# A new order of the attention's matmuls, and a new end of the last layer, in a two-layer decoder trunk

## The chip, the core and the metric

The kernel runs on one core of one Trainium2 chip. TensorE (PE) multiplies, and loads weights beside it (PEld); VectorE (DVE), ScalarE (ACT) and GpSimd (POOL) do the elementwise work; SyncE (SP) issues nearly all transfers. The metric is the device time of one execution in microseconds. A matmul reads its operands from on-chip memory (SBUF) and adds into one of the eight banks of PSUM, 128 partitions of 512 f32 numbers each.

## The reference

All arithmetic is float32, on 1024 tokens of width 1024, in two layers:

```python
def hybrid_layer(x, ...):
    fq, fk, fv, f_logit, rq, rk, rv, rg = split(x @ w_in)
    # 8 forgetting-attention heads of 64: causal softmax, one bias per key and query
    logits = q @ k.T * scale + (c_i[:, None] - c[None, :])
    fox_out = softmax(where(causal, logits, -inf)) @ v
    # 4 retention heads of 128, rotary, chunkwise, group norm, silu gate
    mix = concat([fox_out, ret_out]) @ w_out
    x = layernorm(ALPHA * x + mix, ln1_g, ln1_b)
    ff = square(relu(x @ w_ff1)) @ w_ff2           # 1024 -> 4096 -> 1024
    return layernorm(ALPHA * x + ff, ln2_g, ln2_b)
```

## The kernel before

**Products.** Each f32 operand is split into a high part (`hi`, a cast on ACT) and the rest (`lo`, a subtraction on DVE); a product is three matmuls: lo·hi, hi·lo, hi·hi. The helper `split` (L334 the cast, L335 the subtraction) does it nearly everywhere. Both feed-forward matmuls are done in seven block products (a Winograd form of Strassen's scheme).

**Attention.** For each of 8 heads and 4 query blocks of 256 tokens, three kinds of work stand on PE: F, the scores of one chunk (two matmuls into a `qk` bank, L744; there are two such banks); B, transposes of the probabilities of one pair of key blocks (three or four, L774, into one of two `tr` banks); V, four matmuls of those with the values (L793, into a `pv` bank). Between F and B lie on DVE a fused add and row minimum (`sc,mx<-qk`, L751), on ACT the exponential (L758), on DVE a reciprocal (L760), on POOL the scaling (L761). Between B and V lie the split's cast on ACT and its subtraction on DVE (`pt<-tr` and `pt<-tr,pt`), into three buffers for each part (`PT_BUFS`). X is filler that depends on none of this: three matmuls of the later heads' q and k projection, or of the output projection (L417), or four transposes of retention (L442). PE runs the four kinds in the order that `attention_order()` writes ahead of time, since PE takes its instructions in order and the stage lies in a `manual_schedule` of PE. That function is a small planner with its own clock and its own servers for DVE, ACT and POOL. A piece counts as ready some spare time after its data is expected: `MARGIN` (1.2 us) for B and V, half of it for F. Of the pieces that are ready it takes V, then B, then F, then X; X goes first only while fewer X have been placed than `goal` wants at that count of F (the table `marks`; `FIRST` X ahead of the first F). Both layers use the same order. The order on DVE, ACT and SP is made by the framework's scheduler; there too each engine takes its instructions in order.

**The end.** `feed_forward_out` runs seven products over the same 16 operands each (`PRODUCTS`: 1, 6, 2, 7, 5, 4, 3). `Operands.ahead` loads an operand (two transfers of 256 KB into an `est` buffer; four of these) and splits it into `ehi` and `elo` (rings of six). The last product adds into four banks (`tr`, `tr`, `pv`, `pv`; one for each of the last four token tiles) in groups of `E_GROUP` = 4 operands: four operands for bank 0, the same four for bank 1, and so on. For each of the four token tiles `add` (L1354) then adds the bank to the residual, and `finish` does two `bn_stats` (L1324, one for each half of the row), `bn_aggr` and the norm. `layernorm` (L466): (z − mean)·g on DVE (L469), variance plus epsilon and its power −1/2 on POOL (L471, L473), then times that plus b on DVE (L474). The last token tile has its own `layernorm_halves`, with the row in two halves over ACT, DVE and POOL (L481 to L488). The group order of the last product is not held by `manual_schedule`, so the scheduler may mix groups.

Of the kernel before, what the change touches and what calls it, by code (L numbers as in the profile page):

```python
# [2 lines left out]

# [10 lines left out]
AF = mybir.ActivationFunctionType  # L14
ALU = mybir.AluOpType
# [13 lines left out]
EPS = 1e-5  # L29
# [20 lines left out]
QK_STEPS = 36  # L50
LATE = "WWWWRR" + 6 * "WWR" + 8 * "W"
SLACK = 4
FIRST = 30
LANDING = 9.0
RET_LANDING = 12.0
MARGIN = 1.2


def _consts():
# [31 lines left out]
def attention_order():  # L91
# [35 lines left out]
    rest_from = [never]  # L127

    def goal(f):
        marks = ((0, FIRST), (16, 46), (40, 74), (64, 109), (len(chunks), last_x))  # L130
        for (f0, x0), (f1, x1) in zip(marks, marks[1:]):
            if f <= f1:
                return x0 + (x1 - x0) * (f - f0) / (f1 - f0)
# [7 lines left out]
    while nf < len(chunks) or nb < len(turns) or nv < nb:  # L141
        run(t)
        found = {}
        if nv < nb and nv in pt_ready:
            found["V"] = pt_ready[nv] + MARGIN
            i, jp = turns[nv]
            if jp == 0 and steps[i][1] % 2 == 0:
                found["V"] = max(found["V"], pv_free[(i // 2) % 2])
        if nb < len(turns) and nb - nv < PT_BUFS:
            i, jp = turns[nb]  # L150
            qq = steps[i][1]
            if all((i, rb) in prob for rb in (2 * qq, 2 * qq + 1)):
                found["B"] = MARGIN + max(tr_free[nb % 2], *(prob[(i, rb)] for rb in (2 * qq, 2 * qq + 1)))
        if nf < len(chunks):
            i = chunks[nf][0]
            done = ends[turns[nb][0] - 1] if turns[min(nb, len(turns) - 1)][0] else 0
            if nf - done < DEPTH and (i < 4 or nb >= len(turns) or turns[nb][0] > i - 4) and steps[i][0] in landed:
                found["F"] = MARGIN / 2 + max(qk_free[nf % 2], landed[steps[i][0]])
        if nx < last_x and nx < goal(nf) + SLACK:
            if nx < qk_x:  # L160
                found["X"] = mm_free[(nx // 9) % 2] if nx % 9 == 0 else 0.0
# [91 lines left out]
def hybrid_trunk(ctx: ExitStack, tc, x, w_in, w_out, w_ff1, w_ff2, ln1_g, ln1_b, ln2_g, ln2_b,  # L253
# [222 lines left out]
    def layernorm_halves(z, st, g, b, dst):  # L476
        mv = small([P, 1, 2], "mv")
        V.bn_aggr(mv[:, 0, :], st)
        rs, nb = rstd_of(mv, 1)
        h0, h1 = slice(0, D // 2), slice(D // 2, D)  # L480
        A.activation(z[:, h0], z[:, h0], AF.Identity, bias=nb, scale=rs)  # L481
        V.tensor_scalar(z[:, h1], z[:, h1], rs, nb, op0=ALU.mult, op1=ALU.add)
        V.tensor_tensor(z[:, h1], z[:, h1], g[:, h1], op=ALU.mult)
        G.tensor_tensor(z[:, h0], z[:, h0], g[:, h0], op=ALU.mult)
        V.tensor_tensor(z[:, h1], z[:, h1], b[:, h1], op=ALU.add)
        SP.dma_start(dst[:, h1], z[:, h1])
        V.tensor_tensor(z[:, h0], z[:, h0], b[:, h0], op=ALU.add)
        SP.dma_start(dst[:, h0], z[:, h0])  # L488

    def rows(ap, n):  # L490
        return ap.partition_broadcast(n)
# [719 lines left out]
    class Operands:  # L1211
        def __init__(self, l):
            w2 = w_ff2[l].rearrange("(j m p) (h d) -> j p m h d", m=2, p=P, h=2)
            self.left = {1: 0, 2: 1, 4: 2, 5: 3, 6: 4, 7: 5, 3: 6}
            self.right = {1: lambda j: w2[j][:, 0, 0], 2: lambda j: w2[j][:, 1, 0], 3: lambda j: w2[j][:, 1, 1],
                          4: lambda j: t_d[j][:, 3], 5: lambda j: t_d[j][:, 0], 6: lambda j: t_d[j][:, 1],
                          7: lambda j: t_d[j][:, 2]}
            self.todo = [(p, j) for p in PRODUCTS for j in range(NM // 2)]
            self.ready, self.sent, self.pool = {}, 0, None

        def ahead(self, n):
            while self.sent < min(len(self.todo), n):
                p, j = self.todo[self.sent]
                early = self.sent < 2 * E_EARLY
                if early and self.sent % 4 < 2:
                    st = wp.tile([P, 2, 512], F32, tag="wst", name=nm("est"), bufs=2)
                elif early:
                    if self.sent % 2 == 0:
                        self.two = act.tile([P, 4, 512], F32, tag="act", name=nm("est"))
                    st = self.two[:, 2 * (self.sent % 2) : 2 * (self.sent % 2) + 2, :]  # L1230
                else:
                    st = self.pool.tile([P, 2, 512], F32, tag="est", name=nm("est"), bufs=E_STAGE)
                SP.dma_start(st[:, 0, :], h_d[j][:, self.left[p], :])
                SP.dma_start(st[:, 1, :], self.right[p](j))
                if self.sent < E_EARLY:
                    both = act.tile([P, 4, 512], F32R, tag="act", name=nm("eboth"))
                    hi, lo = both[:, 0:2, :], both[:, 2:4, :]
                elif early:
                    hi = wp.tile([P, 2, 512], F32R, tag="whi", name=nm("ehi"))
                    lo = wp.tile([P, 2, 512], F32R, tag="wlo", name=nm("elo"))  # L1240
                else:
                    hi = self.pool.tile([P, 2, 512], F32R, tag="ehi", name=nm("ehi"), bufs=E_RING)
                    lo = self.pool.tile([P, 2, 512], F32R, tag="elo", name=nm("elo"), bufs=E_RING)
                split(hi, lo, st)
                self.ready[(p, j)] = (hi, lo)
                self.sent += 1
# [5 lines left out]
    def feed_forward_out(l, operands, nxt):  # L1252
# [37 lines left out]
        def triple(ps, i, ops, first, last):  # L1290
            for n, (x_, y) in enumerate(((1, 0), (0, 1), (0, 0))):
                PE.matmul(ps, ops[x_][:, 0, i * P : i * P + P], ops[y][:, 1, :], start=first and n == 0,  # L1292
                          stop=last and n == 2, skip_group_check=True)

        def product(p, ps, first, last, done):
            group = E_GROUP if p == PRODUCTS[-1] else 1
            for j0 in range(0, NJ, group):
                ops = [operands.take(p, j) for j in range(j0, j0 + group)]
                for j in range(j0, j0 + group):
                    if (p, j) in hooks:  # L1300
                        hooks.pop((p, j))(ops[j - j0][0][0:1, :, 0:1].bitcast(F32))
                for i in range(4):
                    for j, o in enumerate(ops):
                        triple(ps[i], i, o, first and j0 + j == 0, last and j0 + j == NJ - 1)
                    if j0 + group == NJ:
                        done(i)
                    if group > 1 or i == 3:
                        tick()
# [11 lines left out]
        def finish(tt):  # L1320
            zt = acc[tt // 2][:, tt % 2, :]
            g, b = last
            for dh in range(2):
                V.bn_stats(stats[:, tt, dh, :], zt[:, 512 * dh : 512 * dh + 512])  # L1324
            if nxt is None and tt == NT - 1:
                layernorm_halves(zt, stats[:, tt], g, b, out[tt * P : tt * P + P, :])
# [77 lines left out]
```

## Time and profile before

| | us |
|---|---|
| median of 3 runs | 2372.41 (2370.77 to 2372.44) |
| profiled execution | 2368.65, of it span 2366.8 |
| PE busy in the span | 2328.8 (98%) |
| DVE, ACT, POOL busy | 1512.2, 1017.7, 396.5 |
| attention, layer 0 and layer 1 | 304.5 to 500 and 1480 to 1676 in the span |
| last product on PE | 2307.1 to 2350.8 |

In the profile PE is all but full, so only stretches in which it has nothing to do can be won, or the tail after its last matmul. A matmul row shows 0.39 us for 512 columns, while the next one starts 0.227 us later (twelve of them take 2.72 us in the chain of waits): the rows overlap by some 0.16 us, and by as much every gap between two rows is too short. "Idle before" is what such a gap is called there.

### The profile page before, as it was taken

What the parts mean: (1) busy time and instruction counts of PE and PEld (TensorE: products, weight loads), DVE (VectorE), ACT (ScalarE), POOL (GpSimd) and SP (SyncE); (2) the same over time, 40 slices, a digit from 0 to 9 for tenths busy, and PEclk for the clock granted to TensorE, in tenths of its full rate; (3) what the DMA queues carried; (4) which work ended last, traced back from release to release, by engine and by line L of the source; (5) the groups of instructions that cost most, each with busy time, mean ns of one, the idle gap of its engine ahead of it and who ended that gap; (6) DMA issues with size and microseconds to landing.
All of it is one profiled execution on the core that took longest, in us unless ns stands there. A gap on an engine that the chain in (4) does not pass through costs nothing.

```text
span 2366.8 us, 32263 instructions
## 1 busy us (share of the span) xinstructions
PE 2328.8 (98%) x11696; PEld 1973.3 (83%) x11696; DVE 1512.2 (64%) x2805; ACT 1017.7 (43%) x1555; POOL 396.5 (17%) x533
## 2 busy tenths in 40 slices
PE   8999999999999999999999999999999999999997
PEld 8888888888888888888898888888888888888885
DVE  4655367756776657655745653777577766676557
ACT  4122256627445444334322222666274454443331
POOL 0232256401000000000202323554000000000003
PEclk9999999999999999999999999999999999999998
DMA  7566776323454458667455667672334544686663
GB/s 251 184 213 210 233 218 200 113 90 126 141 200 175 155 205 297 214 199 236 144 175 196 214 210 243 179 226 87 117 107 162 207 147 147 236 290 219 193 195 142
DMA packets 242159, 443.50 MB, mean 187 GB/s; under 512 B 22080, under 2 KB 126528, under 8 KB 233808
## 3 DMA queue, kind: packets, MB, share of 16 engines
q1 hardware_dynamic: 239696, 433.06, 55.9%
q10 hardware_dynamic: 2304, 8.39, 0.9%
q8 instruction: 92, 1.51, 0.3%
q14 instruction: 67, 0.55, 0.1%
HBM read 302.90 MB, written 138.48 MB: 186 GB/s over the span
## 4 chain that ended last, share of the span: by engine, by line
PE 86%; DVE 4%; DMA 4%; issue 3%; ACT 1%; SPq 1%; POOL 1%; ACTq 0%; DVEq 0%; POOLq 0%
PE mm L417 14%; PE qk L417 10%; PE qk L1082 9%; PE pv L1082 7%; PE tr L1292 7%; PE pv L1292 7%; PE qk L1292 6%; PE mm L1292 6%; PE mm L1082 5%; PE tr L1082 4%; PE pv L793 2%; PE qk L744 2%; PE tr L774 2%; PE tr L417 1%; PE pv L417 1%
## 5 line engine op out<-in xcount | busy, mean ns | idle before, releaser
L335 DVE TENSOR_TENSOR elo<-est,ehi 128x1024 fp32r<-128x1024 f32 x216 | 260.9, 1222 | 180.1 <-ACT ehi L334 179.7
L334 ACT CAST ehi<-est 128x1024 fp32r<-128x1024 f32 x216 | 226.5, 1054 | 342.6 <-PE pv L1292 117.5
L471 POOL TENSOR_SCALAR sd<-mv 128x1 f32<-128x1 f32 x15 | 13.9, 928 | 1202.3 <-DVE mv L468 1202.0
L417 PE MATMUL mm<-whi,act 128*128 128x512 f32 (+1 forms) x656 | 204.0, 373 | 7.6 <-ACT whi L334 5.4
L1082 PE MATMUL qk<-xop,whi 128*128 128x512 f32 x624 | 192.2, 389 | 0.0
L334 ACT CAST whi<-wst 128x512 fp32r<-128x512 f32 (+1 forms) x140 | 115.9, 831 | 158.4 <-DMA wst<-in_w_in_dram 27.4
L417 PE MATMUL qk<-whi,act 128*128 128x512 f32 (+1 forms) x560 | 172.7, 374 | 0.8 <-DVE act L335 0.8
L335 DVE TENSOR_TENSOR wlo<-wst,whi 128x512 fp32r<-128x512 f32 (+1 forms) x140 | 133.3, 954 | 38.4 <-ACT whi L334 37.9
L1082 PE MATMUL pv<-xop,whi 128*128 128x512 f32 x512 | 157.6, 389 | 0.0
L417 PEld LDWEIGHTS mm<-whi,act 128*128 128x128 f32 x656 | 119.8, 190 | 27.4 <-ACT whi L334 5.4
L1082 PEld LDWEIGHTS qk<-xop,whi 128*128 128x128 f32 x624 | 117.1, 188 | 24.2
L1082 PE MATMUL mm<-xop,whi 128*128 128x512 f32 x400 | 123.2, 389 | 0.0
L758 ACT ACTIVATE sc<-sc,mx 128x128 f32<-128x128 f32 (+7 forms) x128 | 99.4, 777 | 53.2 <-DVE mx L751 42.0
L1082 PE MATMUL qk<-xop,wlo 128*128 128x512 f32 x312 | 121.7, 390 | 0.0
L417 PE MATMUL mm<-wlo,act 128*128 128x512 f32 (+1 forms) x328 | 121.3, 370 | 0.0
L335 DVE TENSOR_TENSOR pt<-tr,pt 128x512 fp32r<-128x512 f32 (+1 forms) x160 | 100.7, 632 | 29.0 <-ACT pt L334 27.4
L417 PE MATMUL mm<-act,whi 128*128 128x512 f32 x384 | 119.1, 391 | 0.0
L417 PEld LDWEIGHTS qk<-whi,act 128*128 128x128 f32 x560 | 102.6, 190 | 17.8 <-DVE act L335 1.0
L1082 PEld LDWEIGHTS pv<-xop,whi 128*128 128x128 f32 x512 | 96.1, 188 | 20.0
L761 POOL TENSOR_SCALAR sc<-sc,ri 128x128 f32<-128x128 f32 (+7 forms) x128 | 98.4, 774 | 84.9 <-DVE ri L760 69.7
L334 ACT CAST pt<-tr 128x512 fp32r<-128x512 f32 (+1 forms) x160 | 85.3, 543 | 62.3 <-PE tr L774 61.4
L793 PE MATMUL pv<-pt,vp 128*128 128x256 f32 (+1 forms) x640 | 105.1, 283 | 6.6 <-DVE pt L335 6.6
(286 smaller groups left out, 5929.6 us busy)
## 6 DMA issues: line engine op xcount, KB each, us to landing
est<-h_d SPq DMA_DIRECT2D x224, 256.0 KB, 3.9
wst<-in_w_ff_dram SPq DMA_DIRECT2D x78, 512.0 KB, 4.2
wr<-in_w_ff_dram SPq DMA_DIRECT2D x32, 1024.0 KB, 5.2
t_d<-ts SPq DMA_DIRECT2D x32, 1024.0 KB, 4.3
h_d<-hs SPq DMA_DIRECT2D x32, 1024.0 KB, 5.1
est<-t_d SPq DMA_DIRECT2D x128, 256.0 KB, 3.9
h_d<-rest SPq DMA_DIRECT2D x32, 768.0 KB, 5.5
est<-in_w_ff_dram SPq DMA_DIRECT2D x96, 256.0 KB, 4.9
```

What stands on the lines that cost most here:

```text
L334: A.copy(hi, src)
L335: V.tensor_tensor(lo, src, hi.bitcast(F32), op=ALU.subtract)
L417: PE.matmul(ps, lhs(a, k), rhs(b, k), start=first and i == 0 and j == 0, stop=last and i == n - 1 and j == 2)
L471: G.tensor_scalar(sd, mv[:, :, 1], EPS, 1.0, op0=ALU.add, op1=ALU.mult)
L744: PE.matmul(ps[:, 0:w], qs[:, rb * P : rb * P + P], ks[part][:, c0 : c0 + w], start=part == 0, stop=part == 1)
L758: A.activation(sc[:, 0:ne], sc[:, 0:ne], AF.Exp, bias=mx, scale=-1.0, accum_out=sm)
L761: G.tensor_scalar(sc[:, 0:ne], sc[:, 0:ne], ri, 1.0, op0=ALU.mult, op1=ALU.mult)
L774: PE.transpose(tr[:, 2 * i + rb, :], probs[rb][:, j * P : j * P + P], ident)
L793: PE.matmul(ob[:, c + f * P : c + 256], vp[:, js[i], :], pt[b][:, 2 * i + f : 2 * i + 2, :], start=qq % 2 == 0 and jp == 0 and n == 0 and ...
L1082: PE.matmul(ps, ops[p][a][:, k, :], right[p][b][:, k, :], start=first and k == 0 and n == 0, stop=last and k == 3 and n == 2, skip_group_c ...
L1292: PE.matmul(ps, ops[x_][:, 0, i * P : i * P + P], ops[y][:, 1, :], start=first and n == 0, stop=last and n == 2, skip_group_check=True)
```

## The change

Three things.

1. In the planner each kind has a spare time of its own: F 0.83 us (0.6 before), B 1.54 (1.2), V 2.78 (1.2). `FIRST` is 32 (30), and `goal` wants 57 X by the 16th F (46) and 83 by the 40th (74). The count of matmuls is the same.
2. In the last layer, the last product has groups of 4, 4 and 8 operands in place of four of 4. While the group of eight runs, PE's order is held by `manual_schedule`. The eight operands ahead of the last four are split into one buffer of the pool `act` each (`eboth`) in place of the rings.
3. The norm of the last token tile is written like `layernorm`, with the last step in two halves; ACT's and POOL's share of the row is gone. The `bn_stats` of the first half of tiles 4 to 7 is written further ahead, after product 4.

```diff
-FIRST = 30
+MARK1, MARK2 = 57, 83
+FIRST = 32
-MARGIN = 1.2
+MARGIN_F = 0.83
+MARGIN_B = 1.54
+MARGIN_V = 2.78
...
-        marks = ((0, FIRST), (16, 46), (40, 74), (64, 109), (len(chunks), last_x))
+        marks = ((0, FIRST), (16, MARK1), (40, MARK2), (64, 109), (len(chunks), last_x))
...
-        rs, nb = rstd_of(mv, 1)
-        h0, h1 = slice(0, D // 2), slice(D // 2, D)
-        A.activation(z[:, h0], z[:, h0], AF.Identity, bias=nb, scale=rs)
-        V.tensor_scalar(z[:, h1], z[:, h1], rs, nb, op0=ALU.mult, op1=ALU.add)
-        V.tensor_tensor(z[:, h1], z[:, h1], g[:, h1], op=ALU.mult)
-        G.tensor_tensor(z[:, h0], z[:, h0], g[:, h0], op=ALU.mult)
-        V.tensor_tensor(z[:, h1], z[:, h1], b[:, h1], op=ALU.add)
-        SP.dma_start(dst[:, h1], z[:, h1])
-        V.tensor_tensor(z[:, h0], z[:, h0], b[:, h0], op=ALU.add)
-        SP.dma_start(dst[:, h0], z[:, h0])
+        sd = small([P, 2], "sd")[:, 0:1]
+        G.tensor_scalar(sd, mv[:, :, 1], EPS, 1.0, op0=ALU.add, op1=ALU.mult)
+        rs = small([P, 2], "rs")[:, 0:1]
+        G.tensor_tensor(rs, sd, half[:, 0:1], op=ALU.pow)
+        V.scalar_tensor_tensor(z, z, mv[:, 0, 0:1], g, op0=ALU.subtract, op1=ALU.mult)
+        for h in (slice(D // 2, D), slice(0, D // 2)):
+            V.scalar_tensor_tensor(z[:, h], z[:, h], rs, b[:, h], op0=ALU.mult, op1=ALU.add)
+            SP.dma_start(dst[:, h], z[:, h])
...
-                if self.sent < E_EARLY:
+                if self.sent < E_EARLY or self.closing and 4 < len(self.todo) - self.sent <= E_CLOSE + 4:
                     both = act.tile([P, 4, 512], F32R, tag="act", name=nm("eboth"))
...
-            group = E_GROUP if p == PRODUCTS[-1] else 1
-            for j0 in range(0, NJ, group):
+            sizes = [E_GROUP] * (NJ // E_GROUP) if p == PRODUCTS[-1] else [1] * NJ
+            if nxt is None and p == PRODUCTS[-1]:
+                sizes = [E_GROUP] * ((NJ - E_CLOSE) // E_GROUP) + [E_CLOSE]
...
+                with tc.manual_schedule(engines={mybir.EngineType.PE}) if group == E_CLOSE else nullcontext():
+                    for i in range(4):
+                        for j, o in enumerate(ops):
+                            triple(ps[i], i, o, first and j0 + j == 0, last and j0 + j == NJ - 1)
...
+        if nxt is None:
+            for i in range(4):
+                V.bn_stats(stats[:, i + 4, 0, :], z(1, i, 0)[0])
```

**PE, near the end of layer 0's attention: turn 78 (the 79th of 80 pairs of B and V).** Before, B into `tr_5529` is followed at once by the V ahead of it, by the next B, and by its own V (`pt_5534`, `pt_5535`).

```order
L774 MATMUL tr_5529<-cst,sc_5381 128x128
L774 MATMUL tr_5529<-cst,sc_5411 128x128
L793 MATMUL pv_5486<-pt_5521,vp_4950 128x256
L793 MATMUL pv_5486<-pt_5522,vp_4950 128x256
L793 MATMUL pv_5486<-pt_5521,vp_4950 128x256
L793 MATMUL pv_5486<-pt_5522,vp_4950 128x256
L774 MATMUL tr_5542<-cst,sc_5411 128x128
L774 MATMUL tr_5542<-cst,sc_5381 128x128
L774 MATMUL tr_5542<-cst,sc_5411 128x128
L793 MATMUL pv_5486<-pt_5534,vp_4950 128x256
L793 MATMUL pv_5486<-pt_5535,vp_4950 128x256
```

Now B of the same turn goes into `tr_5525`, and fourteen matmuls of the output projection, the next B and another V stand ahead of its V (`pt_5530`, `pt_5531`).

```order
L776 MATMUL tr_5525<-cst,sc_5407 128x128
L795 MATMUL pv_5494<-pt_5504,vp_4957 128x256
...
L421 MATMUL pv_5597<-wlo_4706,mix_4588 128x512
L421 MATMUL pv_5597<-whi_4705,mix_4588 128x512
L776 MATMUL tr_5538<-cst,sc_5407 128x128
L776 MATMUL tr_5538<-cst,sc_5377 128x128
...
L795 MATMUL pv_5494<-pt_5517,vp_4957 128x256
L795 MATMUL pv_5494<-pt_5518,vp_4957 128x256
...
L795 MATMUL pv_5494<-pt_5530,vp_4957 128x256
L795 MATMUL pv_5494<-pt_5531,vp_4957 128x256
```

What moved: the V of a turn stands further behind its own B. Over the 80 turns of a layer, the pairs with less than 2 us of PE work between the last transpose and the first matmul that reads the `lo` part were 8, and are 1. From a row block's last score to its first transpose, the pairs with under 4.5 us were 2 of 32, and are none. The first eight F had 8 X between them, and have 11; behind the 16th F there were 95 X, and are 85; behind the 64th 33, and are 30.

**PE, the end of the last product.** Before, the last four operands' matmuls are mixed: bank 0 (`tr_20525`) and bank 1 (`tr_20526`) end eighteen and fifteen matmuls before the last; six matmuls of bank 2 and nine of bank 3 (the `pv` banks) stand behind.

```order
L1292 MATMUL tr_20525<-ehi_21369,elo_21370 128x512
L1292 MATMUL tr_20525<-elo_21370,ehi_21369 128x512
L1292 MATMUL tr_20525<-ehi_21369 128x512
L1292 MATMUL tr_20526<-ehi_21369,elo_21370 128x512
L1292 MATMUL tr_20526<-elo_21370,ehi_21369 128x512
L1292 MATMUL tr_20526<-ehi_21369 128x512
L1292 MATMUL pv_20527<-ehi_21362,elo_21363 128x512
```

Now a bank gets all 24 matmuls of the eight operands before the next one starts (`eboth` three matmuls to a row).

```order
L1295 MATMUL tr_20525<-ehi_21365,elo_21366 128x512
L1295 MATMUL tr_20525<-elo_21366,ehi_21365 128x512
L1295 MATMUL tr_20525<-ehi_21365 128x512
L1295 MATMUL tr_20526<-eboth_21261 128x512 x3
L1295 MATMUL tr_20526<-eboth_21267 128x512 x3
L1295 MATMUL tr_20526<-eboth_21273 128x512 x3
L1295 MATMUL tr_20526<-eboth_21279 128x512 x3
L1295 MATMUL tr_20526<-ehi_21344,elo_21345 128x512
```

What moved: bank 0 is complete 72 matmuls before the last, bank 1 48 and bank 2 24.

**DVE, the end of the program.** Before:

```order
L474 SCALAR_TENSOR_TENSOR acc_19401<-acc_19401,rs_21465,lb_20257 128x1024
L1324 BN_STATS stats_19253<-acc_19485 128x6
L469 SCALAR_TENSOR_TENSOR acc_19485<-acc_19485,mv_21484,lg_20256 128x1024
L478 BN_AGGR mv_21508<-stats_19253 128x2
L474 SCALAR_TENSOR_TENSOR acc_19485<-acc_19485,rs_21489,lb_20257 128x1024
L463 SCALAR_TENSOR_TENSOR nb_21514<-mv_21508,rs_21512 128x1
L482 TENSOR_SCALAR acc_19485<-acc_19485,rs_21512,nb_21514 128x512
L483 TENSOR_TENSOR acc_19485<-acc_19485,lg_20256 128x512
L485 TENSOR_TENSOR acc_19485<-acc_19485,lb_20257 128x512
L487 TENSOR_TENSOR acc_19485<-acc_19485,lb_20257 128x512
```

and now:

```order
L478 SCALAR_TENSOR_TENSOR acc_19485<-acc_19485,rs_21472,lb_20257 128x1024
L1363 TENSOR_TENSOR acc_19485<-acc_19485,pv_20528 128x512
L1333 BN_STATS stats_19253<-acc_19485 128x6
L482 BN_AGGR mv_21502<-stats_19253 128x2
L487 SCALAR_TENSOR_TENSOR acc_19485<-acc_19485,mv_21502,lg_20256 128x1024
L489 SCALAR_TENSOR_TENSOR acc_19485<-acc_19485,rs_21506,lb_20257 128x512 x2
```

What moved: the norms of the last four tiles stand one behind the other, each behind its own bank's addition, where those of two tiles at a time were mixed. The `bn_stats` that the source now writes further ahead already stood after product 4 in the scheduler's order, and does not move.

More of the change, by code (lines that the diff above doesn't have):

```diff
@@ L1 @@
-from contextlib import ExitStack
+from contextlib import ExitStack, nullcontext
 from itertools import chain
@@ L38 @@
 E_EARLY = 4
+E_CLOSE = 8
 LEAD = 7
@@ L144, in attention_order @@
         if nv < nb and nv in pt_ready:
-            found["V"] = pt_ready[nv] + MARGIN
+            found["V"] = pt_ready[nv] + MARGIN_V
             i, jp = turns[nv]
@@ L152, in attention_order @@
             if all((i, rb) in prob for rb in (2 * qq, 2 * qq + 1)):
-                found["B"] = MARGIN + max(tr_free[nb % 2], *(prob[(i, rb)] for rb in (2 * qq, 2 * qq + 1)))
+                found["B"] = MARGIN_B + max(tr_free[nb % 2], *(prob[(i, rb)] for rb in (2 * qq, 2 * qq + 1)))
         if nf < len(chunks):
@@ L157, in attention_order @@
             if nf - done < DEPTH and (i < 4 or nb >= len(turns) or turns[nb][0] > i - 4) and steps[i][0] in landed:
-                found["F"] = MARGIN / 2 + max(qk_free[nf % 2], landed[steps[i][0]])
+                found["F"] = MARGIN_F + max(qk_free[nf % 2], landed[steps[i][0]])
         if nx < last_x and nx < goal(nf) + SLACK:
@@ L1219, in __init__ @@
             self.ready, self.sent, self.pool = {}, 0, None
+            self.closing = l == L - 1
         def ahead(self, n):
@@ L1295, in product @@
         def product(p, ps, first, last, done):
-            group = E_GROUP if p == PRODUCTS[-1] else 1
-            for j0 in range(0, NJ, group):
+            sizes = [E_GROUP] * (NJ // E_GROUP) if p == PRODUCTS[-1] else [1] * NJ
+            if nxt is None and p == PRODUCTS[-1]:
+                sizes = [E_GROUP] * ((NJ - E_CLOSE) // E_GROUP) + [E_CLOSE]
+            j0 = -sizes[0]
+            for before, group in zip([sizes[0]] + sizes, sizes):
+                j0 += before
                 ops = [operands.take(p, j) for j in range(j0, j0 + group)]
@@ L1301, in product @@
                         hooks.pop((p, j))(ops[j - j0][0][0:1, :, 0:1].bitcast(F32))
[L1302 to L1308, printed above, removed]
+                with tc.manual_schedule(engines={mybir.EngineType.PE}) if group == E_CLOSE else nullcontext():
+                    for i in range(4):
+                        for j, o in enumerate(ops):
+                            triple(ps[i], i, o, first and j0 + j == 0, last and j0 + j == NJ - 1)
+                        if j0 + group == NJ:
+                            done(i)
+                        if group > 1 or i == 3:
+                            for _ in range(group // E_GROUP or 1):
+                                tick()
         def z(half, i, dh):
@@ L1322, in finish @@
             g, b = last
-            for dh in range(2):
+            for dh in range(0 if nxt is not None or tt < 4 else 1, 2):
                 V.bn_stats(stats[:, tt, dh, :], zt[:, 512 * dh : 512 * dh + 512])
```

## The prediction

> **What bounds the kernel now.** I read the page's busy shares first, then the table by stretches, then who waited for whom on PE in the two attention stretches, and the chain of waits for the end.
>
> ```profile
> span 2366.8 us, 32263 instructions
> PE 2328.8 (98%) x11696; PEld 1973.3 (83%) x11696; DVE 1512.2 (64%) x2805; ACT 1017.7 (43%) x1555; POOL 396.5 (17%) x533
> ```
>
> PE bounds it: 38 us of the span are without a matmul. The stretches that the change touches hold 29 of these (columns: stretch, its length, busy time of PE, PEld, DVE, ACT, POOL, clock, DMA share, GB/s).
>
> ```profile
> 304.50:500.00 195.50, 189.06 (x1176) 167.34 (x1175) 140.00 (x430) 121.56 (x255) 95.83 (x127) 1.00 0.51 148
> 1480.00:1676.00 196.00, 189.43 (x1177) 167.46 (x1176) 140.04 (x430) 122.07 (x255) 94.47 (x127) 1.00 0.50 147
> 2330.00:2367.00 37.00, 20.82 (x92) 16.89 (x90) 20.96 (x27) 3.87 (x4) 8.03 (x9) 0.83 0.26 104
> ```
>
> Attention leaves PE idle for 6.4 us in layer 0 and 6.6 in layer 1. Who ended that idle time (total us, times, longest), layer 0:
>
> ```profile
> PE pv L793 <- DVE pt L335: 3.3, 6, 1.9
> PE tr L774 <- POOL sc L761: 1.4, 2, 1.2
> PE qk L744 <- DVE mx L751: 1.1, 3, 0.6
> PE mm L417 <- DVE act L335: 0.5, 1, 0.5
> ```
>
> Layer 1 gives the same four numbers. So about half is V waiting for its split, then B for POOL's scaling, then F for a score bank. The end is another case. The chain of waits follows PE's last matmuls into DVE and does not come back:
>
> ```profile
> 2339.95 2.72 PE tr L1292 x12
> ...
> 2346.78 1.37 DVE acc L1354 x2
> ```
>
> and PE's last row is
>
> ```profile
> 2350.44 0.39 PE L1292 MATMUL pv<-ehi 128*128 128x512 f32 x1
> ```
>
> PE is through at 2350.83. From there to the end of the span stand 15.97 us in which DVE, POOL and one transfer work off four token tiles.
>
> **The attention order.** It removes no matmul and adds none; it moves V away from its B. What a V needs is seen best near the end of layer 0, where the engines have little else to do:
>
> ```profile
> 493.12 0.60 PE L774 MATMUL tr<-cst,sc 128*128 128x128 f32 x4
> 493.76 0.59 ACT L334 CAST pt<-tr 128x512 fp32r<-128x512 f32 x1 [3.32 <-PE tr L774]
> 494.38 1.25 DVE L335 TENSOR_TENSOR pt<-tr,pt 128x512 fp32r<-128x512 f32 x2 [3.22 <-ACT pt L334]
> 494.40 0.38 PE L793 MATMUL pv<-pt,vp 128*128 128x256 f32 x1
> 495.12 0.74 PE L793 MATMUL pv<-pt,vp 128*128 128x256 f32 x4 [0.34 <-DVE pt L335]
> ```
>
> The last of the four transposes gives way to the next matmul at about 493.5; ACT casts until 494.35, DVE subtracts for 0.65, and the matmul that reads `lo` starts at 495.12: 1.6 us, with empty queues. With a full DVE queue it is more; the longest wait of all is
>
> ```profile
> 365.21 1.22 DVE L335 TENSOR_TENSOR wlo<-wst,whi 128x1024 fp32r<-128x1024 f32 x1
> 366.47 0.69 DVE L807 TENSOR_TENSOR ot<-ot,pv 64x512 f32<-64x512 f32 x1
> 367.19 1.16 DVE L335 TENSOR_TENSOR pt<-tr,pt 128x512 fp32r<-128x512 f32 x2
> 367.94 0.74 PE L793 MATMUL pv<-pt,vp 128*128 128x256 f32 x4 [1.92 <-DVE pt L335]
> ```
>
> where a weight's split and an output's addition stand ahead. Here PE had some 2.8 us of other work and waited about 2 more, so this turn would have needed 4.8. In the compiled order I counted PE's work between B and the `lo` reader, with PE's start-to-start spacing: under 2 us (the 1.6 and a little queue) stood 8 of the 80 V of a layer, now 1; the turn above has 5.4 in place of 2.8. I take seven eighths of the V waits as gone. A wait costs more than its idle time, since the row before it covers 0.16 us of it (0.39 long against 2.72/12 = 0.227): 3.3 + 6 × 0.16 = 4.3 us, so 3.7 won. For B: 1.4 + 2 × 0.16 = 1.7; both pairs under 4.5 us of cover are gone, but POOL's chain is the long one and B now also has more X ahead of it only at the start; I take half, 0.9. For F: 1.1 + 3 × 0.16 = 1.6, and the cover hardly grows; a quarter, 0.4. The wait of X for the retention split (0.5) I leave. That makes 5.0 a layer, **10.0 us** for both. What hides the deferred V is X and F; DVE has 140 of 195.5 us, so it has room. Bounds: nothing won (each wait returns elsewhere), or all of it, 6.3 + 6.5 (layer 1 has 0.2 more in B) + 25 × 0.16 = 16.8 us.
>
> **The end, first part: does PE end at the same time?** It has the same 192 matmuls. Its group of eight starts after 96 of them:
>
> ```profile
> 2307.14 0.39 PE L1292 MATMUL tr<-ehi,elo 128*128 128x512 f32 x1
> ```
>
> 2307.14 + 96 × 0.227 = 2328.9, and then wants a fresh operand every 0.68 us: the eighth by 2333.7. This is the step that can go wrong, since a split takes DVE 1.2 us. In DVE's new order the last split has ten splits, four additions, four `bn_stats`, four `bn_aggr` and five long norm steps from the same addition on that started at 2305.30. That row, and the groups of 2305 to 2347:
>
> ```profile
> 2305.30 0.69 DVE L1354 TENSOR_TENSOR acc<-acc,mm 128x512 f32<-128x512 f32 x1 [1.09 <-PE mm L1292]
> ```
>
> ```profile
> L335 DVE TENSOR_TENSOR elo<-est,ehi 128x1024 fp32r<-128x1024 f32 x12 | 14.4, 1220 | 7.0 <-ACT ehi L334 7.0
> L334 ACT CAST ehi<-est 128x1024 fp32r<-128x1024 f32 x12 | 12.2, 1052 | 24.8 <-DVE acc L474 7.8 <-DMA est<-in_w_ff_dram 5.9 <-PE pv L1292 4.4
> L474 DVE SCALAR_TENSOR_TENSOR acc<-acc,rs,lb 128x1024 f32<-128x1024 f32 x4 | 5.1, 1270 | 0.4 <-POOL rs L473 0.4
> L1324 DVE BATCH_NORM_STATS2 stats<-acc 128x6 f32<-128x512 f32 x4 | 2.6, 676 | 0.0
> L1354 DVE TENSOR_TENSOR acc<-acc,mm 128x512 f32<-128x512 f32 x2 | 1.4, 686 | 1.1 <-PE mm L1292 1.1
> L468 DVE BATCH_NORM_AGGREGATE mv<-stats 128x2 f32<-128x12 f32 x4 | 0.8, 200 | 0.0
> ```
>
> 12.2 + 2.7 + 2.6 + 0.8 + 6.3 = 24.6, so 2329.9 if DVE never waits: 3.8 us early. ACT's ten casts (10.5) fit beside. The transfers stand ahead of all stores of the result in SP's queue now; before, stores stood between them, and ACT waited 5.9 us for transfers. If all 5.9 came back on DVE's path, PE would end 2.1 late. I take 0, and keep 2.1 as a bound. The eight `eboth` buffers and their casts hold nobody up: two of the splits move ahead of that addition, where DVE waits for ACT between splits.
>
> **The end, second part: the tail.** Banks 0 to 2 are complete 16.3, 10.9 and 5.4 us (72, 48, 24 × 0.227) before PE's end. The old tail of the last tile, after the other three, in the timeline:
>
> ```profile
> 2349.26 0.67 DVE L1354 TENSOR_TENSOR acc<-acc,pv 128x512 f32<-128x512 f32 x1
> 2356.04 0.69 DVE L1324 BATCH_NORM_STATS2 stats<-acc 128x6 f32<-128x512 f32 x1
> 2357.83 0.20 DVE L478 BATCH_NORM_AGGREGATE mv<-stats 128x2 f32<-128x12 f32 x1
> 2358.02 1.28 DVE L474 SCALAR_TENSOR_TENSOR acc<-acc,rs,lb 128x1024 f32<-128x1024 f32 x1
> 2358.12 1.23 POOL L459 TENSOR_SCALAR sd<-mv 128x1 f32<-128x1 f32 x1 [1.31 <-DVE mv L478]
> 2359.43 0.55 POOL L461 TENSOR_TENSOR rs<-sd,half 128x1 f32<-128x1 f32 x1
> 2363.08 0.68 DVE L487 TENSOR_TENSOR acc<-acc,lb 128x512 f32<-128x512 f32 x1
> ```
>
> The new chain behind the last matmul: start 0.03, addition 0.60 and `bn_stats` 0.61 (start to start), `bn_aggr` 0.19, (z − mean)·g 1.28; POOL's `sd` ends 0.05 behind that, as at 2359.35 behind DVE's 2359.30; `rs` 0.63 with its start; DVE 0.04 later, two halves of b's step 0.60 + 0.69; and from DVE's end to the span's end as before, 2366.8 − 2363.76 = 3.04 (issue, landing, close). Sum 7.76, against 15.97: **8.2 us** won. The tile before has 0.60 + 0.61 + 0.19 + 1.28 + 0.05 + 0.63 + 0.04 + 1.2 = 4.6 us for its 5.4, so it is out of the way with 0.8 to spare. It is not if POOL's two small steps take what they took when DVE was full of long instructions,
>
> ```profile
> 2311.45 0.19 POOL L471 TENSOR_SCALAR sd<-mv 128x1 f32<-128x1 f32 x1 [571.29 <-DVE mv L468]
> 2320.32 3.03 POOL L471 TENSOR_SCALAR sd<-mv 128x1 f32<-128x1 f32 x1
> 2323.43 2.60 POOL L473 TENSOR_TENSOR rs<-sd,half 128x1 f32<-128x1 f32 x1
> ```
>
> 5.6 us for the pair in place of 1.9; then 2.9 us are lost. With `sd` at its shortest (0.19) both would end inside DVE's 1.28 and 0.7 more is won. I take the row beside DVE's long step, 2358.12, since the new order puts just such a step there. So the end gives 8.2, between 3.2 (5.3 less the 2.1) and 8.9. Moving `bn_stats` costs and brings nothing: it stood there already. ACT's and POOL's share of the last row was on the path and is gone in the sum above.
>
> [...]
>
> **The sum.** 10.0 + 8.2 = 18.2 us. The profiled execution took 2368.65 (span 2366.8 and 1.85 around it) and would take 2350.5. It lies 3.8 below the median of the runs, 2372.41, so I forecast 2372.41 − 18.2 = **2354.2**.
>
> **Rivals.** *The waits only move* (15%): V later means that ring of three buffers, banks and DVE meet elsewhere, and attention stays as it is. For it: B's distance to the `tr` bank's last reader is no longer than before. Against: the short distances of V and B both went down, and none grew shorter. Then 2372.4 − 8.2 = 2364.2. *The group of eight starves* (8%): the last split comes when it came before,
>
> ```profile
> 2339.03 2.36 DVE L335 TENSOR_TENSOR elo<-est,ehi 128x1024 fp32r<-128x1024 f32 x2 [4.27 <-ACT ehi L334]
> ```
>
> at 2341.4; then one pass end and three passes of 5.44 follow, PE ends at 2358.4, the end wins 0.7, and the total is 2361.7. For it: 0.68 us an operand against 1.22; against: the 3.8 us of lead. *Fillers run out* (4%, the other sign): behind the 16th F stand 10 X fewer in a layer, 6.8 us of cover at 0.68. If all of it turns into waits and none of the old ones goes, 13.6 − 8.2 = 5.4 is lost: 2377.8. It decides from 4.1 us a layer on. Against: behind the 64th F 30 X are left of 33, and V's distances there are longer, not shorter. *The planner's order is undone by the scheduler* would fall together with the first; the compiled rows show that it is not.
>
> **How the numbers follow.** 73% for the forecast, with its own range 2346.7 (16.8 + 8.9) to 2362 (half of attention's gain and the end at 5.3). The range to the first two rivals is 2346.5 to 2364.5. About 0.2% (4.7 us) is what a measurement of this kernel can tell from no change. Forecast and the first two rivals are faster by more than that; I leave 4% for a mix of them within it, and 4% slower: faster 92%, same 4%, slower 4%.
>
> **What would show it.** Right: PE's idle time in each attention stretch falls from 6.4 to about 2, with the row `pv <- pt` under 1 us; PE ends the last product without idle time; DVE's last instruction ends 4.7 us behind PE's last matmul. Wrong: a row in which PE waits for `elo` or `eboth` in the last group (starved); `qk <- mx` or `tr <- sc` that grew by as much as `pv` fell (waits moved); long POOL rows between the last two tiles.

## The result

| | before | after |
|---|---|---|
| device time, median of 4 runs each on one chip, us | 2371.59 (2366.98 to 2372.44) | 2352.51 (2350.90 to 2354.48) |
| profiled execution: span, us | 2366.84 | 2352.69 |
| PE's last matmul ends at, us | 2350.82 | 2344.49 |
| from there to the end of the span, us | 16.02 | 8.20 |

The changed kernel is faster: the ratio is 0.9925, with a 95% interval of 0.991 to 0.994. By the medians that is 19.1 us; the two profiled executions lie 14.15 us apart, 6.3 up to PE's end and 7.8 behind it. The profiled execution of before took 2368.65 us, less than its median, and that of the changed kernel 2354.48, the longest of its four. The kernel was timed three times in all, each time beside the kernel before on the same chip, and the medians lay 19.1, 16.1 and 18.1 us apart.

The same lines of the page as were shown of before:

```profile
span 2352.7 us, 32273 instructions
PE 2327.1 (99%) x11696; PEld 1970.4 (84%) x11696; DVE 1514.2 (64%) x2803; ACT 1015.7 (43%) x1554; POOL 389.6 (17%) x532
```

PE is now without a matmul for 25.6 us instead of 38. The table by stretches of the kernel after follows: both attentions from the first F to the last V, the last product, and what lies behind it.

```profile
306.30:497.60 191.30, 187.63 (x1173) 165.31 (x1173) 140.01 (x429) 120.71 (x255) 93.83 (x127) 1.00 0.52 150
1478.10:1669.80 191.70, 187.60 (x1173) 165.35 (x1172) 139.84 (x429) 120.22 (x254) 93.71 (x127) 1.00 0.52 148
2300.60:2344.50 43.90, 43.89 (x194) 36.02 (x192) 38.04 (x44) 9.47 (x10) 16.97 (x14) 1.00 0.48 173
2344.50:2352.70 8.20, 0.00 (x0) 0.00 (x0) 4.29 (x6) 0.00 (x0) 1.83 (x2) 0.78 0.32 128
```

Attention leaves PE idle for 3.7 us in layer 0 and 4.1 in layer 1, where it was 6.4 and 6.6. The last product runs without a gap, so the group of eight does not starve. Who ended PE's idle time in layer 0 (engine and line that waited, whom for, then total us, times, longest):

```profile
PE tr L776 <- POOL sc L763: 1.5, 1, 1.5
PE tr L446 <- DVE pt L339: 0.9, 1, 0.9
PE tr L776 <- DVE ri L762: 0.4, 1, 0.4
PE tr L776 <- DVE pt L339: 0.3, 2, 0.2
PE qk L746 <- DVE mx L753: 0.2, 1, 0.2
```

In layer 1 the first of these rows reads

```profile
PE tr L776 <- POOL sc L763: 2.0, 1, 2.0
```

and the others hardly differ. No V waits any more (3.3 us before). F waits 0.2 instead of 1.1. But B, the row of L776, waits 2.2 us in layer 0 instead of 1.4, and R, the transposes of the retention output at L446, waits 0.9 where it showed no row.

The end, in the timelines of DVE and POOL of the kernel after (start, duration, engine and line, what); PE's last matmul ends at 2344.49:

```profile
2344.52 0.69 DVE L1363 TENSOR_TENSOR acc<-acc,pv 128x512 f32<-128x512 f32 x1 [0.46 <-PE pv L1295]
2345.25 0.69 DVE L1333 BATCH_NORM_STATS2 stats<-acc 128x6 f32<-128x512 f32 x1
2345.97 0.21 DVE L482 BATCH_NORM_AGGREGATE mv<-stats 128x2 f32<-128x12 f32 x1
2346.22 1.28 DVE L487 SCALAR_TENSOR_TENSOR acc<-acc,mv,lg 128x1024 f32<-128x1024 f32 x1
2348.22 1.42 DVE L489 SCALAR_TENSOR_TENSOR acc<-acc,rs,lb 128x512 f32<-128x512 f32 x2 [0.71 <-POOL rs L486]
```

```profile
2346.27 1.28 POOL L484 TENSOR_SCALAR sd<-mv 128x1 f32<-128x1 f32 x1 [3.53 <-DVE mv L482]
2347.64 0.55 POOL L486 TENSOR_TENSOR rs<-sd,half 128x1 f32<-128x1 f32 x1
```

One tile's chain stands behind the last matmul: an addition, `bn_stats`, `bn_aggr`, (z − mean)·g with POOL's pair beside it, and the two halves of b's step. DVE had waited 0.46 us for that last bank, so the other three tiles were done with.

### The profile page after: what moved, and what is told of

The parts are those of the page before. It is cut to its first block, busy times and chain, and to the rows that moved or that the text cites. A ratio compares the mean times of both kernels' runs of the same rounds, so it can differ in the third digit from the quotient of the medians.

```text
span 2352.7 us, 32273 instructions
## 1 busy us (share of the span) xinstructions
PE 2327.1 (99%) x11696; PEld 1970.4 (84%) x11696; DVE 1514.2 (64%) x2803; ACT 1015.7 (43%) x1554; POOL 389.6 (17%) x532
## 4 chain that ended last, share of the span: by engine, by line
PE 88%; issue 4%; DMA 2%; DVE 2%; POOL 2%; ACT 1%; POOLq 0%; ACTq 0%; DVEq 0%; SPq 0%
PE mm L421 15%; PE qk L421 10%; PE qk L1084 9%; PE pv L1084 7%; PE tr L1295 7%; PE pv L1295 7%; PE qk L1295 6%; PE mm L1295 6%; PE mm L1084 5%; PE tr L1084 4%; PE qk L746 3%; PE pv L795 3%; PE tr L776 3%; DMA wr<-in_w_ff_dram 1%; PE tr L421 1%
## 5 line engine op out<-in xcount | busy, mean ns | idle before, releaser
L339 DVE TENSOR_TENSOR elo<-est,ehi 128x1024 fp32r<-128x1024 f32 x208 | 251.5, 1223 | 171.9 <-ACT ehi L338 171.5
L338 ACT CAST ehi<-est 128x1024 fp32r<-128x1024 f32 x208 | 218.5, 1054 | 318.6 <-PE pv L1295 115.5
L1088 ACT ACTIVATE rest<-rest 128x512 f32<-128x512 f32 x96 | 60.5, 631 | 110.4 <-DVE rest L1174 65.1
```

The costliest lines, as they stand in the source:

```text
L338: A.copy(hi, src)
L339: V.tensor_tensor(lo, src, hi.bitcast(F32), op=ALU.subtract)
L1088: A.activation(dst, dst, AF.Relu)
```

## The experiments

Kernels with the same time in the column "before there" ran on one chip, beside those runs of the kernel before. "Behind PE" is the span's end less PE's end in the profiled execution.

| kernel | median us | before there | PE ends at | behind PE |
|---|---|---|---|---|
| order_alone | 2363.93 | 2372.02 | 2346.08 | 16.04 |
| end_alone | 2363.30 | 2372.02 | 2352.76 | 8.22 |
| after_again | 2355.95 | 2372.02 | 2344.51 | 8.21 |
| pool_source | 2354.61 | 2372.02 | 2345.06 | 8.22 |
| old_norm | 2354.96 | 2369.74 | 2343.50 | 9.47 |
| group_four | 2357.45 | 2369.74 | 2345.46 | 11.54 |
| v_margin_12 | 2361.45 | 2369.74 | 2350.94 | 8.22 |
| first_free | 2350.13 | 2369.74 | 2339.86 | 8.20 |
| after_third | 2353.72 | 2371.84 | 2346.10 | 8.21 |
| first_free_2 | 2350.62 | 2371.84 | 2340.14 | 8.20 |
| old_marks | 2360.97 | 2371.84 | 2350.03 | 8.22 |
| first_free_r | 2351.96 | 2371.84 | 2341.43 | 8.22 |

### The two parts apart

*order_alone* has the new order of attention and the old end:

```diff
-FIRST = 30
+MARK1, MARK2 = 57, 83
+FIRST = 32
...
-MARGIN = 1.2
+MARGIN_F = 0.83
+MARGIN_B = 1.54
+MARGIN_V = 2.78
...
```

against the kernel before, with the lines of the planner that use them; the groups, the norm and the places of `bn_stats` are the old ones.

> Only the new attention order, with the end of the kernel before. Theory (the two parts add up, and attention gave 3.2 us a layer in the changed kernel's trace): PE's last matmul ends at about 2344.4 instead of 2350.8, the tail behind it stays 16.0 us, the span is about 2360.4, 6.4 us less than before. The prediction's own term was 10.0. Rival (the order brings nothing, and the earlier end of PE comes from elsewhere): span within 1 us of 2366.8.

*end_alone* has the new end and the old order:

```diff
-MARK1, MARK2 = 57, 83
-FIRST = 32
+FIRST = 30
...
-MARGIN_F = 0.83
-MARGIN_B = 1.54
-MARGIN_V = 2.78
+MARGIN = 1.2
...
```

> Only the new end of the last layer, with the attention order before. Theory: PE's last matmul stays at 2350.8 (the group of eight is not starved), the tail behind it falls from 16.0 to 8.2 us, the span is about 2359.0, 7.8 us less than before (the prediction's term was 8.2). Rival (the group of eight waits for operands, hidden in the changed kernel by the earlier attention): PE's last matmul later than 2351.5, with a wait for elo or eboth.

*after_again* is the changed kernel beside them.

> The changed kernel unchanged, beside its two parts on the same chip. Theory: span 2352.7 as before, 14.1 us less than the kernel before, and equal to the sum of the two parts' gains within 0.5 us. Rival (the parts share a gain): less than the sum by 2 us or more.

The order alone wins 8.1 us by the medians (ratio 0.9965, 0.9952 to 0.9977), the end alone 8.7 (the same ratio and interval), and both together 16.1 (0.9932, 0.9919 to 0.9944). The parts add up within what these medians can tell: 16.8 against 16.1. The stretch behind PE belongs to the end alone (16.04 and 8.22), and an earlier end of PE to the order alone. No sign shows that one part takes anything from the other.

### Is the end's gain the group of eight, or the plain norm?

*old_norm* keeps the group of eight and puts the norm in halves back:

```diff
...
-        V.scalar_tensor_tensor(z, z, mv[:, 0, 0:1], g, op0=ALU.subtract, op1=ALU.mult)
...
+        A.activation(z[:, h0], z[:, h0], AF.Identity, bias=nb, scale=rs)
+        V.tensor_scalar(z[:, h1], z[:, h1], rs, nb, op0=ALU.mult, op1=ALU.add)
...
```

and so on, line by line as before.

> The changed kernel with the old last norm in halves put back (ACT, DVE and POOL share each row), the group of eight kept. Theory: most of the 7.8 us won behind PE's end comes from the group of eight, which leaves one tile's chain there; the old norm's own chain behind the last bank was 5.9 us in the kernel before with POOL's step held beside DVE, some 1.4 longer than the new one's. So from PE's end to the end of the span about 9.6 us (9 to 10.5), against 8.2 with the plain norm. Rival: the plain norm is the main gain, then 12 us or more.

*group_four* keeps the plain norm and the order bank by bank, with a last group of four:

```diff
-                sizes = [E_GROUP] * ((NJ - E_CLOSE) // E_GROUP) + [E_CLOSE]
+                sizes = [E_GROUP] * (NJ // E_GROUP)
...
```

> The changed kernel with the last product's operands in groups of four to the end, the last group still taken bank by bank and the plain norm kept. Banks 0 to 2 are then complete 8.2, 5.4 and 2.7 us before PE's end by the spacing of 0.227 us, each bank's work taking DVE about 4.5. Theory: the tiles queue up on DVE and the stretch from PE's end to the span's end is about 12.5 us (8.2 in the changed kernel, 16.0 before). Rival: the order bank by bank is enough by itself, then 8.2.

Both came out on the theory's side: 9.47 us behind PE with the old norm (9.6 expected), 11.54 with groups of four (12.5 expected). Each is measured with the other part in place: the plain norm is worth 1.3 us, and the group of eight 3.3. That makes 4.6 of the 7.8 us; the other 3.2 come from the two together or from what both runs keep (the last group's order bank by bank, the splits sent earlier, the places of `bn_stats`), and no run here separates them. Groups of four lose because the tiles queue on DVE. In the timeline of group_four, PE's last matmul ends at 2345.46, and DVE still has other tiles to work off:

```profile
2346.10 1.28 DVE L478 SCALAR_TENSOR_TENSOR acc<-acc,rs,lb 128x1024 f32<-128x1024 f32 x1
2347.30 1.28 DVE L473 SCALAR_TENSOR_TENSOR acc<-acc,mv,lg 128x1024 f32<-128x1024 f32 x1
2348.49 0.69 DVE L1333 BATCH_NORM_STATS2 stats<-acc 128x6 f32<-128x512 f32 x1
2349.10 1.27 DVE L478 SCALAR_TENSOR_TENSOR acc<-acc,rs,lb 128x1024 f32<-128x1024 f32 x1
2350.28 0.20 DVE L482 BATCH_NORM_AGGREGATE mv<-stats 128x2 f32<-128x12 f32 x1
```

The last tile's `bn_stats` starts at 2348.49, three microseconds behind the matmul. In the changed kernel it starts 0.76 behind it (2345.25 against 2344.49).

### Which part of the new order removes V's wait?

*v_margin_12* takes back V's margin alone, *old_marks* the marks alone.

```diff
-MARGIN_V = 2.78
+MARGIN_V = 1.2
```

> The changed kernel with V's margin set back to 1.2 us, all else as it is; 7 of 80 V of a layer then have under 2 us of PE's work between B and the reader of the second part (1 in the changed kernel, 8 before). Theory: the wait of V for its split comes back, the row of V behind DVE's split at about 3 us a layer against 0, and PE ends the program 2 to 6 us later (span 2355 to 2359). Rival: V's wait went because of the marks that set how many X stand behind which F; then it stays under 1 us a layer and the span is 2352.7.

```diff
-MARK1, MARK2 = 57, 83
-FIRST = 32
+MARK1, MARK2 = 46, 74
+FIRST = 30
```

> The changed kernel with the marks and the start of X set back (30, 46, 74), the three margins kept. Head 1's bias steps then stand on POOL behind the first scaling, as in the kernel before, since they follow from when X and the first F are issued. Theory: V's wait stays away (its margin is kept), the first B waits about 1.2 us as before, not 1.5 to 2.0, and the R turns wait as in the changed kernel or less; span 2351.5 to 2354. Rival: the marks are what kept F and B supplied in the middle of the layer; without them waits of F or B return at over 2 us a layer and the span is 2355 or more.

PE's waits of v_margin_12 in layer 0; layer 1 has the same row:

```profile
PE pv L795 <- DVE pt L339: 2.8, 6, 0.9
```

So V's wait goes by the margin, as the theory had it, and PE ends the program 6.5 us later than in the changed kernel, a little more than the 2 to 6 expected, at 2350.94, no earlier than before the change. In old_marks no V waits, which the theory also had, and the first wait for POOL is no longer than in the changed kernel. But its span, 2358.25, is the rival's: it is B that waits now.

```profile
PE tr L776 <- DVE pt L339: 3.1, 4, 1.2
PE tr L776 <- POOL sc L763: 1.3, 3, 0.8
```

In layer 1 the first row is 3.4 us. One of its two long waits (the other, 1.2 us, comes at 449) falls in the place where V's longest wait was before, behind a split of a weight and an output's addition in DVE's queue:

```profile
365.80 1.47 DVE L339 TENSOR_TENSOR wlo<-wst,whi 128x1024 fp32r<-128x1024 f32 x1
...
367.70 0.69 DVE L809 TENSOR_TENSOR ot<-ot,pv 64x512 f32<-64x512 f32 x1
...
369.31 0.55 DVE L339 TENSOR_TENSOR pt<-tr,pt 128x384 fp32r<-128x384 f32 x1
```

```profile
369.92 0.66 PE L776 MATMUL tr<-cst,sc 128*128 128x128 f32 x4 [1.11 <-DVE pt L339]
```

The B that starts at 369.92 reuses a `tr` bank, and the split that frees that bank came behind all of this. With the three margins but not the marks, the waits move from V to B: what the first rival of the prediction describes is what happens without the marks. With the marks but not V's margin, V waits nearly as before. Neither half brings 1 us at PE's end (2350.0 and 2350.9 against 2350.8); together they bring 6.3. By the medians, too, the two kernels lie near the new end alone: 8.3 and 10.9 us won, where end_alone won 8.7. So the two work only together. The marks place X earlier, they do not save them up: in the planner's order 85 X stand behind the 16th F in the changed kernel, and 92 in old_marks. Why that spares B its waits, no run here shows.

### Why B's first wait grew

The answer lies in POOL's order at the start of each attention. POOL in the timeline of before, layer 0:

```profile
306.46 0.38 POOL L761 TENSOR_SCALAR sc<-sc,ri 128x128 f32<-128x128 f32 x1 [5.53 <-DVE ri L760]
310.51 0.20 POOL L715 TENSOR_SCALAR ref<-ncb 128x4 f32<-128x4 f32 x1 [3.67 <-DMA ncb<-c_d]
310.68 0.48 POOL L761 TENSOR_SCALAR sc<-sc,ri 128x256 f32<-128x256 f32 x1
```

and of the kernel after:

```profile
311.42 0.20 POOL L717 TENSOR_SCALAR ref<-ncb 128x4 f32<-128x4 f32 x1 [9.87 <-DMA ncb<-c_d]
311.59 0.38 POOL L763 TENSOR_SCALAR sc<-sc,ri 128x128 f32<-128x128 f32 x1
311.94 1.43 POOL L724 TENSOR_SCALAR rel<-ncb,ref 128x256 f32<-128x256 f32 x1
313.46 0.72 POOL L727 TENSOR_TENSOR rel<-rel,cst 128x256 f32<-128x256 f32 x1
314.16 0.48 POOL L763 TENSOR_SCALAR sc<-sc,ri 128x256 f32<-128x256 f32 x1
```

`ref` and `rel` are head 1's bias steps. They wait for the transfer of `ncb`, and head 0's scalings, for which the first B waits, stand behind them in POOL's queue: the second scaling before, both scalings after, with two more bias steps between them. In layer 1 the wait for POOL grew in every profiled execution: 1.6 to 2.0 us in six with the new order (order_alone, old_norm, group_four and the changed kernel three times), 1.2 and 1.3 in the two with the old one. In layer 0 it varies too much to tell: 0.7 to 1.6 against 1.2 and 1.7. Two experiments test the cause. *pool_source* holds POOL to the order of the source:

```diff
-            with tc.manual_schedule(engines={mybir.EngineType.PE}):
+            with tc.manual_schedule(engines={mybir.EngineType.PE, mybir.EngineType.Pool}):
```

> The changed kernel with POOL, too, in the order of the source during attention, so that the bias steps of head 1 no longer stand ahead of the first scalings of head 0. Theory (the first B waits 1.5 and 2.0 us for its scaling because POOL stands in line at the bias step that waits for its transfer): the wait of the first B falls below 0.5 us in both layers, and the span by 2 to 4 us, to about 2349 to 2350.5. Rival (the first B waits because too little work of PE lies ahead of it): its wait stays at 1.5 to 2.0 us. Second rival (the bias steps come too late elsewhere): F waits for them, and the span is not shorter.

The wait for POOL is gone in both layers, and nothing clear of the spread is won (2354.61 against 2355.95, spans 2353.28 and 2352.72). Now DVE waits for bias steps: 1.3 us for `rel` in layer 0, where it waited for none in the changed kernel, and F waits for DVE. PE's waits of pool_source in layer 0, the largest two:

```profile
PE qk L746 <- DVE mx L753: 1.4, 3, 0.6
PE tr L776 <- DVE ri L762: 1.0, 2, 0.5
```

*first_free* moves only the first bias steps. Before head 1's `ncb` is loaded, one number of a scaled score of head 0 is written into its tile; the load then overwrites it:

```diff
+            if h == 1:
+                G.tensor_scalar(ncb[0:1, 0:1], probs[(0, 0)][1][0:1, 0:1], 1.0, 1.0, op0=ALU.mult, op1=ALU.mult)
             SP.dma_start(ncb, rows(c_d[h], P))
```

> The changed kernel, with head 1's bias row loaded into a tile that first takes one number of a scaled score of head 0 (the load then overwrites it, so the result is untouched): head 1's bias steps on POOL can only come behind head 0's first scalings. Theory: the first B of each layer waits for POOL because these bias steps and their transfer stand ahead of the scaling (1.5 us in layer 0, 2.0 in layer 1); that wait falls under 0.5 in both layers, nothing else grows, and the span is 2349.2 to 2350.7 against 2352.7. Rival: the bias steps are then late for head 1's scores, F waits for its score bank as it did with POOL in the order of the source (2.8 us where it was 0.5), and the span is not shorter.

It was run once more, beside the changed kernel:

> The changed kernel once more, beside the next one on the same chip: span 2352 to 2354; the first B of each layer waits 1 to 2.6 us for POOL.

> The kernel with head 1's bias steps behind head 0's first scalings, once more beside the changed kernel. If the 4.6 us of shorter span seen before are the POOL order, the median is 3 to 5 us below that of the changed kernel on this chip and the first B waits for POOL in neither layer. Rival: a part of the 4.6 was the variation of layer 0's attention from one execution to the next; then it is 2 us or less.

POOL in first_free, layer 0:

```profile
307.09 0.38 POOL L765 TENSOR_SCALAR sc<-sc,ri 128x128 f32<-128x128 f32 x1 [6.92 <-DVE ri L764]
309.11 0.48 POOL L765 TENSOR_SCALAR sc<-sc,ri 128x256 f32<-128x256 f32 x1 [1.64 <-DVE ri L764]
309.68 0.18 POOL L716 TENSOR_SCALAR ncb<-sc 1x1 f32<-1x1 f32 x1
...
314.13 0.20 POOL L719 TENSOR_SCALAR ref<-ncb 128x4 f32<-128x4 f32 x1 [0.93 <-DMA ncb<-c_d]
```

Both scalings are done at 309.6 instead of 314.6, no B waits for POOL in either layer, and F's wait stays at 0.2 us. The span is 2348.06 and 2348.34 in the two profiled executions, below the 2349.2 to 2350.7 expected. Of the 4.6 us to the changed kernel's 2352.7, 4.1 lie between the first F and the last V of the two layers (189.2 us in each, in place of 191.0 and 191.4), where waits of 1.5 and 2.0 us are gone. By the medians of one chip the kernel lies 3.1 us below the changed one (2350.62 in 2350.25 to 2351.31, against 2353.72 in 2351.98 to 2356.09); against before its ratio is 0.9912 (0.9898 to 0.9925) and 0.9917 (0.9903 to 0.9932). It is faster than both kernels.

### R's wait

*first_free_r* gives R the margin that B has:

```diff
-                found["X"] = max(tr_free[nb % 2], rest_from[0])
+                found["X"] = max(tr_free[nb % 2] + MARGIN_B, rest_from[0])
```

> The kernel with head 1's bias steps behind head 0's first scalings, and the planner's condition for R (the transposes of the retention output, which use the same banks as B) takes the margin of B where it had none. Theory: R waits 0.9 us a layer for DVE's split of the bank's last reader because no margin stood there; that wait goes, and the span is 1 to 2 us below that of the kernel without this edit. Rival: R is then late and something that waits for R or for a bank waits instead; the span is the same or longer.

The theory fell. R waits no more, but in layer 0 B does:

```profile
PE tr L778 <- DVE pt L339: 1.3, 3, 0.5
PE tr L778 <- DVE act L339: 1.2, 1, 1.2
PE tr L778 <- DVE ri L764: 0.7, 1, 0.7
```

3.2 us in place of 1.8 for all rows of first_free, and PE ends 1.3 us later (2341.43 against 2340.14); the medians lie 1.3 us apart the same way, with ranges that overlap. B now meets R's own split (`act`) in the bank that both share.

## Why the prediction was right, and where it was not

**The total.** 18.2 us were forecast, and the medians gave 19.1, 16.1 and 18.1 in three comparisons; 2354.2 was forecast and 2352.5 measured. The sum was right to about 2 us, and in part by luck. Its term for the end was good, its term for attention too high by some 2 to 4 us. The two profiled executions, from the first of which the sum was made, lie only 14.15 us apart; what the medians show beyond that stands in no term (the last section has a likely source).

**The end** was right in its steps. PE ends the last product without idle time, so the bound of 2.1 us for late operands was not needed. Behind PE stand 8.20 us, where 7.76 were summed up, and 7.8 are won of 8.2. The new chain took 0.73 for the addition where 0.60 was put in, 0.72 for `bn_stats` where it was 0.61, and 0.25 for `bn_aggr` where it was 0.19: in this chain each step needs the one before and starts 0.03 us after its end, while the queued rows that gave the prices belong in part to different tiles and start up to 0.09 us before their predecessor's end. The two halves of b's step took 1.42 where 1.29 was put in. POOL's `sd` took 1.28, as the row beside DVE's long step had said, and DVE's last instruction ends 5.15 us behind PE instead of 4.7. The experiments put 3.3 us on the group of eight and 1.3 on the plain norm, each with the other in place. One row of before was misread without harm to the sum: the addition at 2349.26 is that of the tile before the last (the last tile's starts at 2352.98). And the shortest `sd`, 0.19 us at 2311.45, ran beside a `bn_stats` of DVE (at 2311.28).

**V's wait** was right and too cautious: all of it went, not seven eighths. v_margin_12 shows that the margin is needed, and old_marks that it is enough for V, as the count of PE's work between B and the `lo` reader had said.

**F's wait** fell by 0.9 us of idle time a layer (1.2 with the overlap that the prediction adds), where a quarter, 0.4, was taken; X's 0.5, which was left, went as well.

**B's wait is the step that failed.** It was priced at 0.9 us won a layer, "both pairs under 4.5 us of cover are gone". B lost instead: its rows went from 1.4 to 2.2 us in layer 0 and from 1.6 to 2.6 in layer 1 (1.4 to 2.3 and 2.3 to 2.7 over the six executions of the new order), and R, not in the sum at all, took another 0.9 in each. Two things were missed. The first B does not lack cover on PE; it waits behind another head's bias steps in POOL's queue, which wait for a transfer. That stood in the trace of before at 310.51 and was not read; the new start of X and F moved it from ahead of one scaling to ahead of both (in old_marks, which starts as before, one scaling is ahead of it again), and first_free shows that it holds the wait. And B and R share their banks with the splits that were given more time: a split that V no longer waits for still frees a bank late.

So **attention** won 6.3 us in the profiled executions, of 10.0 forecast. By the second profiled execution of the old order, end_alone, whose PE ends 1.9 us later than before's (2352.76; the dip of its granted clock in the last section, 1.7 us short of the full clock, likely makes most of that, an estimate), it is 8.3, and by the medians of order_alone 8.1. The idle time fell to 3.7 and 4.1 us a layer, not to "about 2". first_free, with B's first wait gone, has PE's end 10.7 and 11.0 us ahead of before's.

**The rivals.** That the group of eight starves is ruled out by the last product's stretch, 43.89 busy of 43.90. That fillers run out did not happen. That the waits only move is false for the change as a whole and true for its parts: old_marks moves V's wait to B, first_free_r R's to B, pool_source POOL's to F.

## What to carry to other kernels

When an engine waits for another, read that other engine's whole queue ahead of the awaited instruction, not only the distance on the waiting engine: one step that waits for a transfer can hold up work that has its data (here the first B, by 1.5 and 2.0 us). More time for one consumer moves others, and the same banks and queues serve them; so a margin and the distribution of filler are tried together, as neither brought much here alone. At the end of a kernel, let the accumulators finish at intervals that are no shorter than the work behind each.

## What the hardware showed that was not expected

**A wait of 2 us on PE can cost more than 2 us.** In order_alone and group_four, the granted clock fell for a while at the start of layer 1's attention. The table by stretches of group_four (the clock is the third number from the end):

```profile
1485.00:1488.00 3.00, 1.20 (x6) 1.21 (x7) 0.17 (x3) 0.48 (x1) 2.83 (x6) 0.85 0.92 280
1488.00:1491.00 3.00, 3.00 (x9) 2.32 (x9) 1.16 (x5) 0.92 (x2) 1.45 (x3) 0.58 0.04 16
```

and of the changed kernel:

```profile
1485.00:1488.00 3.00, 1.08 (x7) 1.04 (x8) 0.49 (x4) 0.48 (x1) 2.83 (x6) 1.00 0.94 279
1488.00:1491.00 3.00, 3.00 (x18) 2.52 (x18) 1.74 (x8) 1.14 (x3) 2.06 (x4) 1.00 0.07 28
```

Both waited 1.97 us for POOL just before, up to 1486.80 and 1486.92. In the one, the granted clock then fell; in the other it did not. Against a full clock, group_four's 0.85 and 0.58 are 1.7 us short in all (0.15 × 3 + 0.42 × 3). A row of one matmul of 512 columns shows 0.63 us there at 1487.79, and the next row starts 0.43 later; in the changed kernel it is 0.39 and 0.23, at 1487.60. order_alone has 0.89 and 0.54 in the same two stretches, 1.7 us short as well. A third case stands in end_alone, where the longest wait of V (1.9 us) was followed by a clock of 0.61 and 0.82 in the stretches from 369 to 375 us, again 1.7 us short. In the attention stretches of the 14 profiled executions, eight such waits of 1.9 to 2.0 us occurred: three were followed by a dip, five were not. No shorter wait there was followed by one; the longest of those is 1.8 us, in old_norm.

What decides whether a dip follows was not shown: the waits of group_four and of the changed kernel are equally long.

Dips are a likely source of spread, and of the part of the gain that the sum does not have. Before has such a wait of V (1.9 us) in both layers, and first_free has none. The profiled execution of before shows no dip (a clock of 1.00 from 9.2 to 2350 us). Of the 28 runs of before that ran beside the experiments, 14 have a mean granted clock of 0.997 and a median of 2370.2 us, and 11 one of 0.996 and a median of 2372.9. The runs of before spread over 4.1 to 7.0 us in these sets, those of first_free over 1.1 and 1.7. But end_alone, with the same two waits of V, spreads over 2.1 only, and that the dips make up the difference was not shown.

**A full DVE did not by itself stretch POOL's step.** In group_four, DVE's rows follow each other without a gap from 2341.04 to 2350.48. Among them `sd` took 0.19 us beside `bn_stats` (at 2343.72) and beside the addition L1363, which reads `acc` and a bank (at 2345.64). Beside L487, which reads `acc` and `lg`, it took 1.28, and so it did in the changed kernel beside L473, which reads the same two (at 2335.39 and 2340.83):

```profile
2345.64 0.19 POOL L475 TENSOR_SCALAR sd<-mv 128x1 f32<-128x1 f32 x1 [1.09 <-DVE mv L472]
...
2350.57 1.28 POOL L484 TENSOR_SCALAR sd<-mv 128x1 f32<-128x1 f32 x1 [4.12 <-DVE mv L482]
```

What in DVE's step makes the difference, no run here varied. In the new tail DVE starts 0.05 us ahead of POOL (2346.22 and 2346.27), and then waits 0.71 us for `rs`. That an `sd` of 0.19 would bring both of POOL's steps inside DVE's 1.28, as the prediction has it, the trace of before does not bear out: there two `sd` took 0.46 us together from 2350.14, ahead of L469 at 2350.60, and the two `rs` behind them, from 2350.68, took 2.79 together, most of it beside L469, where one takes 0.55 in the new tail. With `sd` ahead of the long step, the new tail was not tried.
